# One layer of a diffusion backbone on one core: in the projections with features on partitions, the order of high-part and low-part products within a weight tile

## The chip, the core and the metric

The kernel runs on one core of a Trainium2 chip. Time is device microseconds of one launch; that of the kernel before is the median of three runs. Beside it stands one execution taken by the hardware profiler, from which every duration below is read. The engines are TensorE (PE, with its weight loads PEld), VectorE (DVE), ScalarE (ACT), GpSimd (POOL) and SyncE (SP), which here only issues transfers.

## The reference, cut to what matters

One layer: adaLN (shift, scale and gate from a condition vector), neighbourhood attention over 256 latent tokens and 256 context tokens, output projection, then a gated FFN with a convolution over three tokens; D = 2048, 16 heads, FFN width 5504, all in float32. Only the latent stream is the output.

```python
def conv_ffn(h, w_up, conv_w, conv_b, w_down):
    gate, up = jnp.split(dwconv3(h @ w_up, conv_w, conv_b), 2, axis=-1)
    return (jax.nn.silu(gate) * up) @ w_down

def reference(x, c, ctx, ...):
    sh1, sc1, g1, sh2, sc2, g2 = adaln(cond_lat, w_ada, b_ada)
    h = modulate(rms_norm(x, norm_mix_g), sh1, sc1)
    hc = modulate(rms_norm(ctx, norm_mix_g), csh1, csc1)
    y = neighbourhood_attention(h, hc, w_qkv, q_g, k_g, rpb, w_o, False)
    x = x + g1 * y
    hf = modulate(rms_norm(x, norm_ffn_g), sh2, sc2)
    return x + g2 * conv_ffn(hf, w_up, conv_w, conv_b, w_down)
```

The attention ends with a product with `w_o`. The three products that the change touches are those with `w_o` (2048 x 2048), `w_up` (2048 x 11008) and `w_down` (5504 x 2048).

## The kernel before

**Products in high and low parts.** Every operand of these products is split into an exact high and an exact low part of 12 bits each, and a product of two operands is hi·hi + hi·lo + lo·hi. Activations lie with features on partitions: a block of 128 features holds 512 columns, the 256 tokens' high parts and beside them their low parts. One *wide* product (line 728) multiplies the weight's high part with all 512 columns; one *narrow* product (line 732) multiplies the weight's low part with the 256 columns of high parts, and adds to the first half of the same PSUM bank. One bank belongs to one block of 128 output features.

**Weight tiles.** A tile is 256 rows (two blocks k of 128) by up to 512 columns (four blocks b). `wload` (line 139) has SyncE issue its transfer into one of four slots `wr`; `wpair` (lines 147 to 161) has ScalarE copy it to the rounded high part `wh` (line 155, three slots) and VectorE subtract that from the raw tile to give the low part `wl` (line 156, two slots). `plan` lists all tiles in the order of use; `ahead` (line 180) keeps up to two split, and `weight` hands out the next. So a new `wl` can be written when the tile two before has had its last narrow product.

**The loops.** `proj` (lines 713 to 737) goes over the tiles of a column chunk; within a tile it runs over b, then k, and writes the wide product and then the narrow one. With `fold`, which the last chunk of 256 columns in `w_o` and `w_down` has, the wide product is written as two of 256 columns into the same sums. Three callers: the output projection (the list `WO`; 24 tiles of 512 columns and 16 of 256), the FFN's first product (11 column chunks for the gate and 11 for the up half in turn, 8 tiles each, 160 of them 512 columns wide) and the FFN's second product (the list `DOWN`: three chunks of 512 columns and two of 256, 22 tiles each, the last tile of a chunk with one block k). The banks go round through eight: two `ms`, four `pj`, two `mx`.

**Work beside it.** After each tile `tick` hands out pieces of other work. In the FFN's first product these are the pieces of the chunk before, for each of its four banks: out of PSUM (`drop`, line 828 on VectorE), convolution (lines 838 and 842) and gating (line 855); and the sums of adaLN's last gate (`ada_tasks`), in which ScalarE scales a tile (276) and GpSimd adds it up (277, two sums of 128x512 a tile), or VectorE does both (279). In the second product the pieces are `finish`: two additions and an output transfer for each bank of the finished chunk.

**What sets the order.** The program order is only the start. A scheduler with a model of the times fixes each engine's final order: it lets instructions pass whose inputs it believes ready and holds back others. The slots of the pools set the rest. `hold` makes the first splits of the FFN wait for the second normalization.

Of the kernel before, what the change touches and what calls it, by code (L numbers as in the profile page):

```python
# [15 lines left out]
P = 128  # L16
D = 2048
T = 256
# [9 lines left out]
# pieces of attention per weight tile of the projections beside it  # L28
RATE, RATE3 = 0.46, 0.36
# slots of adaLN weight tiles  # L30
# [4 lines left out]
# columns of the packed small operands  # L35
# [5 lines left out]
# column chunks of the FFN's second product  # L41
DOWN = [(0, 512), (512, 512), (1024, 512), (1536, 256), (1792, 256)]
# blocks of 128 features of the first normalization in steps: (first, number)
GRAINS = [(0, 1), (1, 1)] + [(k, 2) for k in range(2, 16, 2)]
# output projection: (column, columns, first block, last block), the heads of group 3 behind the others
# [5 lines left out]
def block_kernel(  # L51
# [13 lines left out]
    nc = tc.nc  # L65
# [17 lines left out]
    def at():  # L83
        """The four banks of attention in turn."""
        turns.append(0)
        return (ms, mx)[len(turns) % 2]()

    # ---------------------------------------------------------------- constants
# [8 lines left out]
    # window mask over key columns; query column = partition % 64  # L97
    maskt = cp.tile([P, GRID], F32, name="maskt")
    nc.gpsimd.memset(maskt, 0.0)
    for half in range(2):  # L100
        rows = slice(GRID * half, GRID * half + GRID)
        lo = maskt[rows, 0 : GRID - WIN]
# [16 lines left out]
    # adaLN columns by 128-row block: shift / scale of each stream, gates  # L119
# [7 lines left out]
    # relative position rows, each repeated so that a row pitch of 30 shifts it by one column  # L127
# [4 lines left out]
    # ---------------------------------------------------------------- helpers  # L132
    def wload(src, k0, kn, c0, cn, pool=None):
        """Rows of 128-blocks k0..k0+kn and columns c0..c0+cn of a weight."""
# [12 lines left out]
    def wpair(src, k0, kn, c0, cn):  # L147
        """The same rows and columns as exact high and low parts, 12 bits each."""
# [14 lines left out]
    # every weight tile in the order of its use, the next one split ahead of the current one's use  # L163
# [16 lines left out]
    def ahead():  # L180
        """Splits up to two tiles."""
        while plan and len(split) < 2:
            split.append((plan[0], wpair(*plan.popleft())))

    def weight(*tile_):
        """The split parts of the plan's next weight tile."""
        ahead()
        spec, pair = split.popleft()
        assert spec[1:] == tile_[1:]
        return pair  # L190

    def rsqrt_newton(pool, v, n, name, bufs=2):
        """v ** -0.5 for a [P, n] tile, refined once."""
# [11 lines left out]
    def rstd_rows(pool, sums, name, copy):  # L205
        """Sums of squares, [token, block of tokens] -> rstd of each token on every partition."""
# [16 lines left out]
    def col_sums(sums, parts):  # L223
        """sums[t, b]: the sum over partitions of the parts' column b * 128 + t."""
# [9 lines left out]
    class Pieces(deque):  # L234
        """Work handed out in pieces between the products of another part."""
# [16 lines left out]
    def ada_tasks(pool, i, c, dst, gcol=None):  # L252
        """Latent adaLN columns i*D + 512c..: dst[:, 4c..4c+3] = value + b, or (1 + value + b) * g.

        Pairs of a load and its use, and the sum over partitions as a last step: every third tile is
        summed on DVE, the others are scaled on ACT and summed on Pool.
        """
# [45 lines left out]
    def ada_pieces(cols):  # L303
        """Those of several chunks as pieces: loads two tiles ahead, each sum a tile behind."""
# [20 lines left out]
    # ================================================================ attention  # L325
# [29 lines left out]
    def stats(xin, name):  # L355
        """rstd of the tokens of a stream, on every partition."""
# [13 lines left out]
    def nat(psl, tt0, w, kt0, n, first, last):  # L370
        """psl[i] += h[tile tt0 + i, n k-blocks from kt0] @ (split weights), tokens on partitions."""
# [18 lines left out]
    # shift and scale of both streams in steps of one or two 128-row blocks; the first products  # L390
    # of group 0 follow each step
# [3 lines left out]
    def ada_step(b0, nb, work=()):  # L395
        """Blocks b0..b0+nb of the shifts and scales, a piece of the given work ahead of every load."""
# [43 lines left out]
    def modulate(b0, nb, streams=None):  # L440
        """The normalized, scaled and shifted blocks b0..b0+nb as high and low parts."""
# [14 lines left out]
    # sums over steps of the v products of groups 0 and 1  # L456
    vsums = [kv.tile([P, 4, CH], F32, tag=tag, name="vsum") for tag in ("qq", "kl")]

    def first_products(b0, nb):
        """Products with the blocks b0..b0+nb, in six pieces: k of group 0, v of groups 0 and 1."""  # L460
# [54 lines left out]
    def norm_transpose(pt, gcol, dh, dl, t0):  # L515
        """Per-head RMS norm of a [tokens, 4 x 128] product, transposed and split."""
# [55 lines left out]
    def bias(h):  # L572
        """Bias and window of head h: partition = query column, slot = row offset, key column."""
# [16 lines left out]
    def attention(g, q, k, v):  # L590
        """The heads of group g in pieces: scores and softmax, transposes, weighted sums."""
# [86 lines left out]
    def out_of_psum(pts, dst):  # L678
        """The tiles of a projection, where they wait for the end of the group before."""
# [24 lines left out]
    v = []  # L704
# [7 lines left out]
    # ---------------------------------------------------------------- features on partitions  # L712
    def proj(src, kn, c0, cn, mov, tick, k_lo=0, k_hi=None, pts=None, fold=False):
        """src[:, c0:c0+cn].T @ activations: one [128, hi*w | lo*w_hi] bank per 128 columns.

        With fold, the two halves go into the same sums.
        """
        nb = cn // P
        pts = pts or [pj() for _ in range(nb)]
        for k0 in range(k_lo, k_hi or kn, KT):  # L720
            n = min(KT, kn - k0)
            wh, wl = weight(src, k0, n, c0, cn)
            for b in range(nb):
                bs = slice(b * P, (b + 1) * P)
                for k in range(n):
                    kt = k0 + k
                    for t0, t1 in ((0, T), (T, 2 * T)) if fold else ((0, 2 * T),):
                        nc.tensor.matmul(  # L728
                            pts[b][:, : t1 - t0], wh[:, k, bs], mov(kt, slice(t0, t1)),
# [228 lines left out]
```

## Time and profile before

| | |
|---|---|
| time, median of three runs | 1455.89 us (1454.18 to 1458.64) |
| span of the profiled execution | 1455.1 us |
| TensorE busy, products | 1405.5 us, 97%, 7608 products |
| TensorE busy, weight loads | 1166.9 us, 80% |
| VectorE / ScalarE / GpSimd busy | 69% / 54% / 20% |
| HBM | 217 GB/s over the span |
| output projection | from 600 to 705 us |
| second normalization | from 705 to 718 us |
| FFN, first product | from 718 to 1207 us |
| FFN, second product | from 1207 to 1456 us |

A product is recorded from its start to its modelled end, and the next one starts before that end. Rows of the timeline group products of one kind that follow each other (x4 is four); the time of such a row runs from the first one's start to the last one's end. How much TensorE does in a stretch is therefore read from starts, not from busy time. A wait in brackets, as [0.30 <-DVE wl L156], is idle time ahead of the row and the instruction that ended it.

### The profile page before, as it was taken

The numbers are of one execution on the slowest core, as the hardware profiler recorded it, in microseconds if no ns is written. First come the engines' busy times: TensorE is split into PE (matmuls) and PEld (weight loads), VectorE is DVE, ScalarE is ACT, GpSimd is POOL, SyncE is SP. The second block draws the span as 40 slices with busy tenths as digits, with TensorE's granted clock in tenths as the row PEclk, the third lists the DMA queues.
The fourth block names the chain that finished last, engine by engine and source line by source line (L and its number), as shares of the span: only waits on it lengthen the run. The fifth ranks groups of instructions, "written<-read, shape, count | busy, mean of one in ns | idle before, by whom it ended". The sixth has DMA issues, their size and how long they took to land.

```text
span 1455.1 us, 21097 instructions
## 1 busy us (share of the span) xinstructions
PE 1405.5 (97%) x7608; PEld 1166.9 (80%) x7608; DVE 1004.8 (69%) x1541; ACT 782.6 (54%) x1356; POOL 285.2 (20%) x208
## 2 busy tenths in 40 slices
PE   5999999999998999999899999999999999999998
PEld 2665787778787887788788888888888888888888
DVE  4556587687868778766868878788777775545454
ACT  4322265676565676664656656666665654333333
POOL 1000025465445556200201111111111000000000
PEclk9999999999999999999899999999999999999999
DMA  9999547687667777445567776777776556566554
GB/s 308 357 329 319 176 141 250 199 260 220 213 222 246 223 247 244 151 152 175 183 193 230 224 238 222 244 219 228 233 230 193 183 175 206 185 202 205 167 170 156
DMA packets 208920, 317.14 MB, mean 218 GB/s; under 512 B 23360, under 2 KB 87744, under 8 KB 208816
## 3 DMA queue, kind: packets, MB, share of 16 engines
q1 hardware_dynamic: 208688, 315.79, 68.1%
q8 instruction: 59, 0.97, 0.3%
q14 instruction: 45, 0.37, 0.1%
q10 hardware_dynamic: 128, 0.01, 0.0%
HBM read 312.75 MB, written 3.01 MB: 217 GB/s over the span
## 4 chain that ended last, share of the span: by engine, by line
PE 66%; DVE 12%; issue 10%; DMA 7%; ACT 2%; POOL 2%; SPq 1%; DVEq 0%; POOLq 0%; ACTq 0%
PE pj L728 15%; PE pj L732 8%; PE mx L728 7%; PE ms L728 6%; DVE wl L156 4%; PE pj L379 4%; PE pj L378 4%; PE pj L380 4%; DMA wa<-in_w_ada 4%; PE mx L732 4%; PE ms L732 3%; PE ms L411 2%; PE mx L378 2%; PE mx L379 2%; PE mx L380 2%
## 5 line engine op out<-in xcount | busy, mean ns | idle before, releaser
L156 DVE TENSOR_TENSOR wl<-wr,wh 128x1024 fp32r<-128x1024 f32 (+2 forms) x425 | 496.1, 1168 | 257.0 <-PE pj L732 86.8
L155 ACT CAST wh<-wr 128x1024 fp32r<-128x1024 f32 (+2 forms) x425 | 411.8, 970 | 406.0 <-PE pj L728 150.5
L277 POOL TENSOR_TENSOR acc<-acc,wa 128x512 f32<-128x512 f32 x144 | 226.6, 1573 | 440.9 <-issue 218.1
L728 PE MATMUL pj<-hf,wh 128*128 128x512 f32 x688 | 226.7, 397 | 2.0 <-DVE hf L818 2.0
L379 PE MATMUL pj<-wl,hh 128*128 128x512 f32 x512 | 204.8, 400 | 4.6 <-DVE wl L156 4.5
L380 PE MATMUL pj<-wh,hl 128*128 128x512 f32 x512 | 202.0, 397 | 0.0
L378 PE MATMUL pj<-wh,hh 128*128 128x512 f32 x512 | 194.4, 400 | 2.5 <-ACT hh L450 2.5
L732 PE MATMUL pj<-hf,wl 128*128 128x256 f32 x688 | 154.7, 284 | 2.2 <-DVE wl L156 1.7
L732 PEld LDWEIGHTS pj<-hf,wl 128*128 128x128 f32 x688 | 130.6, 190 | 20.6 <-DVE wl L156 6.2
L728 PEld LDWEIGHTS pj<-hf,wh 128*128 128x128 f32 x688 | 125.3, 190 | 17.7 <-DVE hf L818 2.8
L276 ACT ACTIVATE wa<-wa,sT 128x512 f32<-128x512 f32 x144 | 97.4, 718 | 77.7 <-DMA wa<-in_w_ada 68.1
L728 PE MATMUL mx<-hf,wh 128*128 128x512 f32 x352 | 124.1, 393 | 0.0
L379 PEld LDWEIGHTS pj<-wl,hh 128*128 128x128 f32 x512 | 97.8, 191 | 28.7 <-DVE wl L156 7.9
L728 PE MATMUL ms<-hf,wh 128*128 128x512 f32 x336 | 120.1, 396 | 0.0
L378 PEld LDWEIGHTS pj<-wh,hh 128*128 128x128 f32 x512 | 96.8, 190 | 27.0 <-ACT hh L450 3.4
L380 PEld LDWEIGHTS pj<-wh,hl 128*128 128x128 f32 x512 | 97.6, 191 | 19.5
L732 PE MATMUL mx<-hf,wl 128*128 128x256 f32 x352 | 84.8, 282 | 1.5 <-DVE wl L156 1.5
L279 DVE SCALAR_TENSOR_TENSOR acc<-wa,sT,acc 128x512 f32<-128x512 f32 x80 | 74.4, 931 | 10.7 <-DMA wa<-in_w_ada 10.1
L732 PE MATMUL ms<-hf,wl 128*128 128x256 f32 x336 | 81.7, 282 | 0.0
L732 PEld LDWEIGHTS mx<-hf,wl 128*128 128x128 f32 x352 | 66.3, 188 | 10.4 <-DVE wl L156 3.2
L732 PEld LDWEIGHTS ms<-hf,wl 128*128 128x128 f32 x336 | 63.3, 188 | 7.8
L728 PEld LDWEIGHTS ms<-hf,wh 128*128 128x128 f32 x336 | 63.2, 188 | 6.9
(251 smaller groups left out, 2384.7 us busy)
## 6 DMA issues: line engine op xcount, KB each, us to landing
wr<-in_w_up SPq DMA_DIRECT2D x160, 512.0 KB, 4.4
wa<-in_w_ada SPq DMA_DIRECT2D x128, 512.0 KB, 4.7
wr<-in_w_qkv SPq DMA_DIRECT2D x93, 512.0 KB, 4.9
wr<-in_w_down SPq DMA_DIRECT2D x63, 512.0 KB, 4.6
wx<-in_w_ada SPq DMA_DIRECT2D x56, 512.0 KB, 8.7
wr<-in_w_o SPq DMA_DIRECT2D x24, 512.0 KB, 3.8
wr<-in_w_down SPq DMA_DIRECT2D x45, 256.0 KB, 3.0
wr<-in_w_up SPq DMA_DIRECT2D x16, 384.0 KB, 3.4
```

The source lines that it names most:

```text
L155: a = nc.scalar.copy(hi[:, :kn, :cn], w[:, :kn, :cn])
L156: b = nc.vector.tensor_tensor(out=lo[:, :kn, :cn], in0=w[:, :kn, :cn], in1=hi[:, :kn, :cn].bitcast(F32), op=ALU.subtract,)
L276: nc.scalar.mul(w[:, k, :], w[:, k, :], s)
L277: nc.gpsimd.tensor_add(acc, acc, w[:, k, :])
L279: nc.vector.scalar_tensor_tensor(out=acc, in0=w[:, k, :], scalar=s, in1=acc, op0=ALU.mult, op1=ALU.add)
L378: nc.tensor.matmul(pt, hh[:, kt, ts], wh[:, k, :], start=a, stop=False)
L379: nc.tensor.matmul(pt, hh[:, kt, ts], wl[:, k, :], start=False, stop=False)
L380: nc.tensor.matmul(pt, hl(kt, ts), wh[:, k, :], start=False, stop=z)
L411: nc.tensor.matmul(ap_[32 * k : 32 * k + 32, :n], s32[:, 4 * q + k, :], w[:, k * n : (k + 1) * n], start=(q == 0), stop=(q == 3), tile_pos ...
L728: nc.tensor.matmul(pts[b][:, : t1 - t0], wh[:, k, bs], mov(kt, slice(t0, t1)), start=(kt == 0 and t0 == 0), stop=False,)
L732: nc.tensor.matmul(pts[b][:, :T], wl[:, k, bs], mov(kt, slice(0, T)), start=False, stop=(kt == kn - 1),)
```

## The change

In `proj`, the loop over the cells of a tile is run twice: first all wide products of the tile (for each b, both k), then all narrow ones in the same order of cells. Operands, sums, banks, splits, transfers and `tick` stay. The rest of the diff blanks comments, which moves line numbers by one behind `proj`: the wide product is line 727 afterwards, the narrow one 733, `drop` 829, the convolution 839 and 843, the gating 856.

```diff
     def proj(src, kn, c0, cn, mov, tick, k_lo=0, k_hi=None, pts=None, fold=False):
...
             wh, wl = weight(src, k0, n, c0, cn)
-            for b in range(nb):
-                bs = slice(b * P, (b + 1) * P)
-                for k in range(n):
-                    kt = k0 + k
-                    for t0, t1 in ((0, T), (T, 2 * T)) if fold else ((0, 2 * T),):
-                        nc.tensor.matmul(
-                            pts[b][:, : t1 - t0], wh[:, k, bs], mov(kt, slice(t0, t1)),
-                            start=(kt == 0 and t0 == 0), stop=False,
-                        )
+            cells = [(b, slice(b * P, (b + 1) * P), k) for b in range(nb) for k in range(n)]
+            for b, bs, k in cells:
+                kt = k0 + k
+                for t0, t1 in ((0, T), (T, 2 * T)) if fold else ((0, 2 * T),):
                     nc.tensor.matmul(
-                        pts[b][:, :T], wl[:, k, bs], mov(kt, slice(0, T)), start=False,
-                        stop=(kt == kn - 1),
+                        pts[b][:, : t1 - t0], wh[:, k, bs], mov(kt, slice(t0, t1)),
+                        start=(kt == 0 and t0 == 0), stop=False,
                     )
+            for b, bs, k in cells:
+                kt = k0 + k
+                nc.tensor.matmul(
+                    pts[b][:, :T], wl[:, k, bs], mov(kt, slice(0, T)), start=False,
+                    stop=(kt == kn - 1),
+                )
             tick()
```

**Three places in the built order.** In these rows the names are the program's tiles: `hf` is the FFN's input, `act_*` the activated features, `pj`, `ms` and `mx` the banks; x4 is four such instructions in a row.

TensorE, FFN's first product, where one chunk ends in its `pj` banks and the next begins in `mx` and `ms`. Before:

```order
L728 MATMUL pj<-hf,wh 128x512 x4
L728 MATMUL mx<-hf,wh 128x512 x2
L728 MATMUL ms<-hf,wh 128x512 x2
L732 MATMUL pj<-hf,wl 128x256
L728 MATMUL pj<-hf,wh 128x512
L732 MATMUL pj<-hf,wl 128x256 x2
L728 MATMUL pj<-hf,wh 128x512
```

After:

```order
L727 MATMUL pj<-hf,wh 128x512 x8
L727 MATMUL mx<-hf,wh 128x512
L733 MATMUL pj<-hf,wl 128x256 x8
L727 MATMUL mx<-hf,wh 128x512 x3
L727 MATMUL ms<-hf,wh 128x512 x4
L733 MATMUL mx<-hf,wl 128x256 x4
L733 MATMUL ms<-hf,wl 128x256 x4
```

Before, the scheduler had moved four wide products of a tile ahead and let the others alternate with the narrow ones; now all eight stand ahead of the eight narrow ones.

VectorE, FFN's first product, from the split of one tile of a chunk (`wl_9318`) to that of the next (`wl_9350`). Before:

```order
L156 TENSOR_TENSOR wl_9318<-wr_9315,wh_9317 128x1024
L842 SCALAR_TENSOR_TENSOR y_9337<-z_9308,sm_69,y_9337 128x255
L838 SCALAR_TENSOR_TENSOR y_9373<-z_9312,sm_69,y_9373 128x255
L828 TENSOR_TENSOR z_9403<-ms_9054,t_9402 128x256
L855 TENSOR_TENSOR y_9337<-y_9337,gt_9169 128x256
L838 SCALAR_TENSOR_TENSOR y_9428<-z_9370,sm_69,y_9428 128x255
L842 SCALAR_TENSOR_TENSOR y_9373<-z_9312,sm_69,y_9373 128x255
L156 TENSOR_TENSOR wl_9350<-wr_9347,wh_9349 128x1024
```

After:

```order
L156 TENSOR_TENSOR wl_9318<-wr_9315,wh_9317 128x1024
L839 SCALAR_TENSOR_TENSOR y_9337<-z_9308,sm_69,y_9337 128x255
L829 TENSOR_TENSOR z_9403<-ms_9054,t_9402 128x256
L843 SCALAR_TENSOR_TENSOR y_9337<-z_9308,sm_69,y_9337 128x255
L839 SCALAR_TENSOR_TENSOR y_9373<-z_9312,sm_69,y_9373 128x255
L839 SCALAR_TENSOR_TENSOR y_9428<-z_9370,sm_69,y_9428 128x255
L856 TENSOR_TENSOR y_9337<-y_9337,gt_9169 128x256
L156 TENSOR_TENSOR wl_9350<-wr_9347,wh_9349 128x1024
```

Six pieces stand between the two splits in both; they are two 838, two 842, one 828 and one 855 before, and three 839, one 843, one 829 and one 856 now.

TensorE, FFN's second product, the hand-over from its third chunk of columns (`pj`) to its fourth (`mx`). Before:

```order
L728 MATMUL pj<-act_fp,wh 128x512 x4
L728 MATMUL mx<-act_row_6466,wh 128x512 x2
L732 MATMUL pj<-act_fp,wl 128x256 x4
L732 MATMUL mx<-act_row_6466,wl 128x256
L728 MATMUL mx<-act_row_6466,wh 128x512
L732 MATMUL mx<-act_row_6466,wl 128x256 x2
```

After:

```order
L727 MATMUL pj<-act_fp,wh 128x512 x4
L727 MATMUL mx<-act_row_6466,wh 128x512 x3
L733 MATMUL pj<-act_fp,wl 128x256 x4
L727 MATMUL mx<-act_row_6466,wh 128x512
L733 MATMUL mx<-act_row_6466,wl 128x256 x4
```

The old chunk's last four narrow products stand behind three wide ones of the next chunk instead of two.

## Rows read from the trace of the kernel before

**Rows 1.** Page, part 1: busy us (share of the span) x instructions.

```profile
PE 1405.5 (97%) x7608; PEld 1166.9 (80%) x7608; DVE 1004.8 (69%) x1541; ACT 782.6 (54%) x1356; POOL 285.2 (20%) x208
```

**Rows 2.** Windows: stretch; its us; busy of PE, PEld, DVE, ACT, POOL; PEclk; DMA; GB/s.

```profile
718.00:1207.00 489.00, 485.30 (x2757) 420.49 (x2756) 382.06 (x557) 301.06 (x470) 63.68 (x40) 1.00 0.68 214
```

**Rows 3.** Timeline of TensorE, 903.6 to 908.9: start us, us, instruction [idle before].

```profile
903.66 1.08 PE L728 MATMUL pj<-hf,wh 128*128 128x512 f32 x4
904.58 0.28 PE L732 MATMUL pj<-hf,wl 128*128 128x256 f32 x1
904.69 0.40 PE L728 MATMUL pj<-hf,wh 128*128 128x512 f32 x1
...
906.47 1.08 PE L728 MATMUL pj<-hf,wh 128*128 128x512 f32 x4
907.86 0.39 PE L732 MATMUL pj<-hf,wl 128*128 128x256 f32 x1 [0.30 <-DVE wl L156]
908.08 0.40 PE L728 MATMUL pj<-hf,wh 128*128 128x512 f32 x1
```

**Rows 4.** Waits of weight loads by stage (us, times, longest); the last from their timeline.

```profile
PEld ms L732 <- DVE wl L156: 1.4, 2, 0.8
...
PEld pj L732 <- DVE wl L156: 6.2, 10, 0.9
PEld mx L732 <- DVE wl L156: 3.2, 4, 0.8
...
PEld mx L732 <- DVE wl L156: 1.6, 3, 0.6
...
907.86 0.19 PEld L732 LDWEIGHTS pj<-hf,wl 128*128 128x128 f32 x1 [0.74 <-DVE wl L156]
```

**Rows 5.** Timeline of VectorE, 901 to 907.

```profile
901.12 1.22 DVE L156 TENSOR_TENSOR wl<-wr,wh 128x1024 fp32r<-128x1024 f32 x1
902.26 1.52 DVE L842 SCALAR_TENSOR_TENSOR y<-z,sm,y 128x255 f32<-128x255 f32 x1
903.70 1.51 DVE L838 SCALAR_TENSOR_TENSOR y<-z,sm,y 128x255 f32<-128x255 f32 x1
905.14 0.41 DVE L828 TENSOR_TENSOR z<-ms,t 128x256 f32<-128x256 f32 x1
905.48 0.41 DVE L855 TENSOR_TENSOR y<-y,gt 128x256 f32<-128x256 f32 x1
905.81 0.47 DVE L838 SCALAR_TENSOR_TENSOR y<-z,sm,y 128x255 f32<-128x255 f32 x1
906.20 0.47 DVE L842 SCALAR_TENSOR_TENSOR y<-z,sm,y 128x255 f32<-128x255 f32 x1
906.60 1.21 DVE L156 TENSOR_TENSOR wl<-wr,wh 128x1024 fp32r<-128x1024 f32 x1
```

**Rows 6.** Timeline of GpSimd, 900 to 908.

```profile
901.28 3.66 POOL L277 TENSOR_TENSOR acc<-acc,wa 128x512 f32<-128x512 f32 x2 [19.42 <-issue]
```

**Rows 7.** Timeline of TensorE in the second FFN product, 1265 and 1408.

```profile
1265.40 1.09 PE L728 MATMUL pj<-act_fp,wh 128*128 128x512 f32 x4
1266.33 0.64 PE L732 MATMUL pj<-act_fp,wl 128*128 128x256 f32 x4
1266.81 0.63 PE L728 MATMUL mx<-act_row,wh 128*128 128x512 f32 x2
...
1408.33 0.63 PE L728 MATMUL mx<-act_fp,wh 128*128 128x512 f32 x2
...
1409.75 0.63 PE L728 MATMUL mx<-act_fp,wh 128*128 128x512 f32 x2
```

**Rows 8.** Timeline of TensorE, 895.2 to 897.6: eight wide products, then a narrow one.

```profile
895.26 0.62 PE L728 MATMUL mx<-hf,wh 128*128 128x512 f32 x2
...
897.10 0.28 PE L732 MATMUL mx<-hf,wl 128*128 128x256 f32 x1
```

**Rows 9.** Timeline of TensorE, 1397 to 1401.

```profile
1399.56 0.73 PE L728 MATMUL mx<-act_row,wh 128*128 128x512 f32 x2 [0.96 <-ACT wh L155]
```

## The prediction, made before the result was known

> **What bounds the kernel now.** I read the page first: TensorE is busy 97% of the span with 7608 products [rows 1], and the windows by stage say the same of the long stage of the FFN's first product: 485 of 489 us, with the granted clock at full speed and VectorE at 382 us [rows 2]. Ends of products are modelled, so this busy time hides short stalls. I therefore read TensorE by the starts in its timeline: how far one product starts behind the one before.
>
> A tile of this stage has eight wide products (512 columns, high part) and eight narrow ones (256 columns, low part); the scheduler has put four wide ones ahead. In the tile that starts at 903.66 nothing waits: the first narrow product comes 0.92 us behind the first wide one (0.23 us a product), the next product 0.11 us later, the next tile 2.81 us later [rows 3]. That next tile, at 906.47, is the same, but its first narrow product comes 1.39 us behind, held by the VectorE instruction that makes the low part (L156), and the product behind it takes 0.22 instead of 0.11 [rows 3]. This stall costs 0.47 + 0.11 = 0.58 us. The waits of the weight loads count such places: 2 in the output projection (1.4 us), 10 and 4 in the first FFN product (6.2 and 3.2), 3 in the second (1.6); the one of 906.47 stands there as 0.74 us [rows 4]. So a recorded wait is worth 0.58/0.74 = 0.78 of itself: 16 places and 10.8 us ahead of the second FFN product are 8.4 us of TensorE, the other three 1.2 us.
>
> Why VectorE is late: [rows 5] are its instructions from one split to the next. The split for the tile of 906.47 stands, in VectorE's order, behind six pieces of the chunk before. Two of these took 1.52 and 1.51 us, where the same kind takes 0.47, while GpSimd ran two sums of adaLN [rows 5, 6]. So 4.3 us pass between the end of one split (902.34) and the start of the next (906.60).
>
> **The change part by part.** Nothing is added or removed: the same products, loads, splits and transfers. The order moves.
>
> *The low part is wanted later.* The built order has eight wide products, then eight narrow ones, so the first narrow one comes at 8 x 0.23 = 1.84 us of its tile instead of 0.92. What else VectorE may do between two splits follows: from the end of the tile that frees the first split's buffer there are two tiles (5.62 us) and then 0.92 or 1.84 us to the need, and two splits take 2 x 1.22. That leaves 4.1 us now and 5.0 us after. [Rows 5] need 4.3, and the first split started at 901.12, 0.27 us behind its tile's start (906.47 - 5.62 = 900.85): 0.47 us late, as the products say. After the change VectorE's order has three L838, one L842, one L828 and one L855 between the same two splits: 4 x 0.47 + 2 x 0.41 = 2.7 us, and with two sums of GpSimd among them 2 x 1.05 more, 4.8 us. With the 0.27 that is 5.1 against 5.0: it just fits, within a tenth. The other places now wait as long or less (at most 0.9 us recorded, 0.7 by the ratio) and gain the same 0.92 us. I take 90% of the 8.4 us: **-7.5 us**. Bounds: half stays, -4.2; all goes, -8.4. What is late next in these stages is only the products' own spacing.
>
> The Trainium skill speaks to the 1.05 us (SBUF — State Buffer, "Who interferes with whom"): a VectorE instruction with two SBUF inputs contends with a GpSimd instruction that reads SBUF, and the one that starts first holds the shared pair for its whole length while the other fully blocks. The trace agrees in kind: 1.52 and 1.51 us where 0.47 is usual. By that rule the change takes none of these blocks away, it only leaves time to suffer them, and a third one between two splits would cost its full length again, which is the slower rival below.
>
> *Spacing.* Does a group of eight cost what the alternation costs where nothing waits? A tile of one block in the second FFN product already runs four wide and then four narrow: 1265.40 to 1266.81 is 1.41 us, 0.48 of it for the four narrow ones [rows 7]. The same number of each in alternation takes 1408.33 to 1409.75, 1.42 us [rows 7]. Where two tiles meet, eight wide ones follow each other, 20 times, in 1.82 to 1.84 us (895.26 to 897.10) [rows 8]. A grouped tile is then 1.83 + 2 x 0.48 = 2.79 us against 2.80 to 2.81. I take -13 ns. There are 24 such tiles in the output projection, 160 in the first FFN product, 63 in the second: 247 x 13 ns = **-3.2 us**. Bounds: 1.84 + 0.97 = 2.81, nothing; and, if narrow ones come nearer to the 0.11 us of a single one [rows 3], 0.118 each, 1.83 + 0.94 = 2.77, -10 us. I stay by the runs of four, which are closest to a run of eight.
>
> The Trainium skill (TensorE: Matmul & The Clock Gate, "Back-to-back issue gap") makes the gap a matter of the product's own columns, N/2.4 + 2.5 ns, 216 and 109 ns here, whatever stands beside it; the trace has about 230 and 120. By that rule this term is zero and the sum is -7.2 us.
>
> *The second FFN product.* Its three short stalls stand where a finished chunk of four banks is handed over; a little behind them TensorE waits 0.96 us for the ACT split of a tile that had not landed [rows 9]. VectorE's eight additions of the finished chunk start when its banks are done, and on SyncE's queue the output transfers and the next weight loads follow these. The built order has three wide products of the next chunk ahead of the old chunk's last narrow ones where two stood: the banks are done 0.23 us later. The three stalls are covered, but the wait for the landing takes their place. I put it at **+0.3 us**; bounds -2.2 (all of it goes: 1.2 and 1.0) and +1.
>
> *At no cost.* The high part's buffer comes back earlier by the eight narrow products; ACT's split had time already, so nothing follows. The low part's buffer comes back at the tile's end, as now, so VectorE's splits, the slots of the raw weights and their transfers keep their times. A finished chunk's banks are dropped later, but the next chunk has four others. The kernel's last tile stands as before, and all of TensorE's order ahead of the output projection is unchanged.
>
> Sum: -7.5 - 3.2 + 0.3 = -10.4 us. Against the profiled execution's span, 1455.1, that is 1444.7; the median of the three runs, 1455.9, lies 0.8 us above the span, so **1445.5 us**.
>
> **The rivals.**
> - *Order is free.* A tile takes the same time in either order, and only the waits go: 1455.9 - 7.5 + 0.3 = 1448.7 us. For it: 1.41 against 1.42 us is one last digit [rows 7]. Against it: wide products come at 0.23 in a run of eight at most [rows 8], and between narrow ones no closer [rows 3]. The Trainium skill's rule on gaps above is this case.
> - *The lateness moves along.* The pieces between two splits leave a tenth of a microsecond; every further wait for ACT among them makes the split late again. Then 70% of the stalls stay: 1455.9 - 2.5 + 0.3 is 1453.7 without a gain from spacing, about 1451 with it; I price it at 1453. For it: the 5.1 against 5.0 above.
> - *Slower.* A third sum of GpSimd falls between the splits of a chunk's third and fourth tile: 2.7 + 3 x 1.05 = 5.9 us, 0.9 over the 5.0 from which it decides, and 0.1 for the product behind. At 22 chunks that is +22 us; less 8.4 and 3.2 it gives 1466 us. For it: drops and convolutions now stand closer together there. Against it: the sums come in pairs, 19.42 us of idle time apart [rows 6], and not every chunk has one there.
> - *More.* Narrow products at 0.118 us and a free hand-over: 1455.9 - 8.4 - 10 - 2.2 = 1435 us. Against it: 0.48 us for four [rows 7].
> That the change does nothing is excluded: the built order is different in every tile.
>
> **How the numbers follow.** A difference under about 0.3% (4.4 us, so a time over 1451.5) can't be told from no change. Forecast 0.54 (1441 to 1450), order is free 0.15, moving along 0.16, slower 0.07, more 0.08. Faster by over 0.3%: nearly all of the first two and "more", with a little of "moving along", 0.75; within it: the rest, 0.18; slower: 0.07. The range 1439 to 1453.5 leaves out the slower case, most of "more" and the upper end of "moving along", together not quite 0.2.
>
> **What would show it.** Right: the waits of the low part's weight loads on L156 fall from 12.4 us to under 2.5; from a tile's first wide product to its first narrow one it is 1.84 us nearly everywhere; tiles start 2.79 us apart. Spacing wrong: undisturbed tiles at 2.81 or more, or near 2.77. Moving along: waits on L156 of the old size, behind 1.9 us or more of wide products. Slower: three VectorE instructions lengthened by 1 us between two splits. The prediction is wrong altogether if eight narrow products in a row take clearly more than 0.96 us, or if ACT's or VectorE's splits wait for something that isn't in these rows.

## The result, and the profile after

The changed kernel takes **1447.6 us** (median of eight runs, 1445.9 to 1449.9), the one before 1455.0 beside it (eight runs, 1452.0 to 1458.6). The ratio is 0.9945, with a 95% interval of 0.9929 to 0.9962: 8.0 us, and between 5.5 and 10.3. The forecast was 1445.5, 10.4 us less.

The profiled execution's span fell from 1455.1 to 1444.0 us, by 11.1, which is more than the medians say. The timeline of TensorE tells where. I divide it at the first product that reads `om` (output projection), `hf` (first FFN product) and `act` (second), and at the end of its last product:

| us | up to the output projection | to the FFN | first FFN product | second FFN product |
|---|---|---|---|---|
| before | 603.5 | 109.4 | 492.0 | 246.5 |
| after | 601.0 | 110.6 | 484.6 | 244.2 |
| difference | -2.6 | +1.2 | -7.4 | -2.3 |

The FFN's first product starts at 712.9 us before, earlier than the 718 of the table of stages before. The first column is the same order of TensorE's instructions in both kernels. In the eleven other executions below with that order (e8 alone has another) it took 599.9 to 607.1 us: the 2.6 us are scatter. What the change did is in the other three columns, -8.5 us, and that agrees with the runs.

The boundary between the two FFN products does not part equal work. When the first product that reads `act` runs, the old order still has three wide and six narrow products of the first FFN product to come, 1.40 us by their starts; the grouped order has six narrow ones, 0.71 us; e4, e7 and e10 have none. TensorE there, before and then after:

```profile
1204.94 1.08 PE L728 MATMUL pj<-act_row,wh 128*128 128x512 f32 x4
...
1207.15 0.28 PE L732 MATMUL ms<-hf,wl 128*128 128x256 f32 x1
```

```profile
1196.11 1.52 PE L727 MATMUL pj<-act_row,wh 128*128 128x512 f32 x6
...
1197.94 0.40 PE L733 MATMUL ms<-hf,wl 128*128 128x256 f32 x2
```

*On equal work*, with these counted where they belong, the first FFN product takes 493.4 and 485.3 us, 8.1 less, and the second 245.1 and 243.5, 1.6 less. Stage times below go by the first product, as in the expectations, unless they are called on equal work.

The page of the profile after, part 4 (the chain that ended last, by engine):

```profile
PE 74%; issue 9%; DMA 5%; DVE 4%; ACT 3%; POOL 2%; SPq 1%; DVEq 0%; POOLq 0%; ACTq 0%
```

TensorE is busy 97% of the span as before [rows 1], which says next to nothing. The chain says more: VectorE holds 4% of it, where it held 12%. The waits of the weight loads after, for the output projection, the first and the second FFN product (us, times, longest):

```profile
PEld ms L733 <- DVE wl L156: 0.8, 1, 0.8
...
PEld mx L733 <- DVE wl L156: 0.4, 1, 0.4
...
PEld mx L733 <- DVE wl L156: 1.1, 3, 0.5
PEld mx L727 <- ACT wh L155: 0.4, 1, 0.4
```

On L156 they were 1.4, 9.4 and 1.6 us [rows 4]; now they are 0.8, 0.4 and 1.1. A place like that of [rows 3, 5, 6], after: TensorE, VectorE and GpSimd in their timelines.

```profile
896.31 2.00 PE L727 MATMUL pj<-hf,wh 128*128 128x512 f32 x8
898.15 1.12 PE L733 MATMUL pj<-hf,wl 128*128 128x256 f32 x8
899.10 2.00 PE L727 MATMUL pj<-hf,wh 128*128 128x512 f32 x8
900.94 1.11 PE L733 MATMUL pj<-hf,wl 128*128 128x256 f32 x8
```

```profile
896.51 2.33 DVE L156 TENSOR_TENSOR wl<-wr,wh 128x1024 fp32r<-128x1024 f32 x1
```

```profile
894.57 3.19 POOL L277 TENSOR_TENSOR acc<-acc,wa 128x512 f32<-128x512 f32 x2 [19.16 <-issue]
```

From the first wide product to the first narrow one it is 1.84 us, and from tile to tile 2.79. GpSimd's pair still lengthens VectorE: here it hits the split itself, 2.33 us where 1.21 is usual. The split ends at 898.84; its tile's low part is first wanted at 900.94. The delay is still there, and nobody waits for it.

Here only one instruction of VectorE was lengthened: three `drop`s, which read a bank, ran beside GpSimd's pair at 0.38 to 0.41 us each. The tightest places of the stage have two lengthened pieces between two splits. VectorE at one of them, and the weight load that wants the low part:

```profile
906.61 1.51 DVE L843 SCALAR_TENSOR_TENSOR y<-z,sm,y 128x255 f32<-128x255 f32 x1
908.04 1.51 DVE L858 TENSOR_TENSOR act_row<-y,act_row 128x256 fp32r<-128x256 f32 x1
...
910.14 1.21 DVE L156 TENSOR_TENSOR wl<-wr,wh 128x1024 fp32r<-128x1024 f32 x1
...
911.89 1.13 PEld L733 LDWEIGHTS pj<-hf,wl 128*128 128x128 f32 x8
```

The split ends at 911.35, 0.54 us before that load starts. In the whole stage the kernel before has 12 places with two instructions lengthened from the end of one split to the end of the next (the second split may be one of them), and the weight load waits at all 12. The changed kernel has 8, and the low part is done 0.5 to 2.1 us ahead of its load at each.

### The profile page after: what moved, and what is told of

It is laid out like the page before. It is cut to its first block, busy times and chain, and to the rows that moved or that the text cites. A ratio compares the mean times of both kernels' runs of the same rounds, so it can differ in the third digit from the quotient of the medians.

```text
span 1444.0 us, 21091 instructions
## 1 busy us (share of the span) xinstructions
PE 1399.1 (97%) x7608; PEld 1167.8 (81%) x7608; DVE 1000.0 (69%) x1541; ACT 778.5 (54%) x1356; POOL 281.1 (19%) x208
## 4 chain that ended last, share of the span: by engine, by line
PE 74%; issue 9%; DMA 5%; DVE 4%; ACT 3%; POOL 2%; SPq 1%; DVEq 0%; POOLq 0%; ACTq 0%
PE pj L727 18%; PE pj L733 9%; PE mx L727 8%; PE ms L727 7%; PE pj L379 5%; PE pj L378 5%; PE pj L380 5%; PE mx L733 4%; PE ms L733 4%; DMA wa<-in_w_ada 3%; PE ms L411 2%; PE mx L378 2%; PE mx L379 2%; PE mx L380 2%; POOL acc L277 2%
## 5 line engine op out<-in xcount | busy, mean ns | idle before, releaser
L156 DVE TENSOR_TENSOR wl<-wr,wh 128x1024 fp32r<-128x1024 f32 (+2 forms) x425 | 503.8, 1186 | 280.6 <-PE pj L733 106.3
L727 PE MATMUL pj<-hf,wh 128*128 128x512 f32 x688 | 176.3, 396 | 2.0 <-DVE hf L819 2.0
L733 PEld LDWEIGHTS pj<-hf,wl 128*128 128x128 f32 x688 | 94.6, 192 | 6.8
L733 PE MATMUL pj<-hf,wl 128*128 128x256 f32 x688 | 97.8, 285 | 0.0
L727 PE MATMUL mx<-hf,wh 128*128 128x512 f32 x352 | 97.7, 394 | 0.0
L727 PE MATMUL ms<-hf,wh 128*128 128x512 f32 x336 | 90.9, 390 | 0.0
L727 PEld LDWEIGHTS mx<-hf,wh 128*128 128x128 f32 x352 | 60.6, 190 | 7.8
L478 DVE TENSOR_TENSOR vsum<-vsum,mx 128x512 f32<-128x512 f32 x64 | 43.2, 684 | 34.2 <-PE mx L380 34.0
L733 PEld LDWEIGHTS mx<-hf,wl 128*128 128x128 f32 x352 | 53.7, 189 | 7.1 <-DVE wl L156 0.4
L584 POOL TENSOR_TENSOR bt<-bt,maskt 128x384 f32<-128x384 f32 x16 | 17.9, 1123 | 206.4 <-DMA bt<-rpd 173.7
```

The source lines that it names most:

```text
L156: b = nc.vector.tensor_tensor(out=lo[:, :kn, :cn], in0=w[:, :kn, :cn], in1=hi[:, :kn, :cn].bitcast(F32), op=ALU.subtract,)
L478: nc.vector.tensor_add(acc[:, h0 + i, :], acc[:, h0 + i, :], pr_[i])
L727: nc.tensor.matmul(pts[b][:, : t1 - t0], wh[:, k, bs], mov(kt, slice(t0, t1)), start=(kt == 0 and t0 == 0), stop=False,)
L733: nc.tensor.matmul(pts[b][:, :T], wl[:, k, bs], mov(kt, slice(0, T)), start=False, stop=(kt == kn - 1),)
```

## Experiments

### Taking GpSimd's sums away: e1 and e2

The theory (A): the stalls come from VectorE's pieces, lengthened while GpSimd adds, and the later need covers them; besides, the new order itself is some 13 ns a tile cheaper. The rival (B): the order of the products is what costs. Both kernels lose the same line:

```diff
                 elif pool_:
                     nc.scalar.mul(w[:, k, :], w[:, k, :], s)
-                    nc.gpsimd.tensor_add(acc, acc, w[:, k, :])
+                    if i != 5:
+                        nc.gpsimd.tensor_add(acc, acc, w[:, k, :])
```

> The kernel before, with GpSimd's sums of adaLN's last gate left out (line 277 for this gate alone; its transfers, ScalarE's scaling and VectorE's sums stay, so that the gate is incomplete). TensorE's order is that of before. Theory A (two terms: VectorE's splits are late in the first FFN product because GpSimd's sums lengthen its pieces, some 6 us; and the grouped order has 15 ns less a tile): weight loads wait on L156 under 1.5 us in the first FFN product instead of 9.4; that stage takes 486 us instead of 492; tiles stay 2.81 us apart; time about 1449. Theory B (the order of the products is what costs, and the splits are late whatever GpSimd does): waits of 7 us or more remain, the stage takes 490 or more, time 1453 to 1456.

> The changed kernel with the same sums left out. Theory A: next to e1_before_no_sums only the spacing is left: first FFN product 2.3 us shorter than there (160 tiles x 15 ns), second some 1.5 to 2 us, time about 3.5 us less, near 1446; next to the changed kernel with its sums no more than 0.5 us in the first FFN product. Theory B: 7 us or more below e1_before_no_sums.

e1 took 1450.1 us (ratio 0.9955, 0.9938 to 0.9972). Its first FFN product took 485.6 us, and the waits on L156 there fell from 9.4 to 1.0:

```profile
PEld pj L733 <- DVE wl L156: 1.0, 2, 0.8
```

One of VectorE's two kinds of convolution pieces in this stage (count, busy us, mean ns), first in the kernel before, then in e1, where the lines are one further; the other kind has 578 and 479 ns:

```profile
L838 DVE SCALAR_TENSOR_TENSOR y<-z,sm,y 128x255 f32<-128x255 f32 x83 | 46.8, 576 | 0.6 <-ACT y L835 0.6
```

```profile
L839 DVE SCALAR_TENSOR_TENSOR y<-z,sm,y 128x255 f32<-128x255 f32 x83 | 38.7, 479 | 1.7 <-ACT y L836 1.6
```

The same instructions take 479 ns on average instead of 577 when GpSimd does not add, and the stalls go with that. TensorE's order is that of before, word for word, so B falls. e2 took 1446.2 us. Its first FFN product is 483.3 us, 2.3 less than e1 (3.0 on equal work): the rest of the stalls, the spacing, and 0.6 us in the stage's first 7 us. Next to the changed kernel it is 1.3 less, where 0.5 at most was expected. Of that, 1.1 us lie in those first 7 us. Behind the second normalization the granted clock is still 0.50 (1.2 GHz), in e2 for the first 3.4 us of the stage, in the changed kernel for the first 5.8. The second FFN product of e2 was not 1.5 to 2 us shorter than e1's but 0.2 (245.3 and 245.4), and on equal work it was 0.5 longer: in e2 a weight load waits 1.5 us there for ScalarE's split, in e1 none does.

### More of the same: e11 and e12

Each of the same sums made twice (the loop around the line is `for _ in range(1 + (i == 5))`), in the changed kernel and in the one before; one execution each.

> The changed kernel with each of GpSimd's sums of adaLN's last gate made twice (the gate is then wrong; everything else, and TensorE's order, stays). Asks how much room the later need leaves. By the prediction's account there is a tenth of a microsecond between two splits with two lengthened pieces; with four, 2 x 1.05 us more, the split would be 2 us late at each of the places that were stalls before: weight loads wait on L156 15 to 30 us in the first FFN product, which takes 500 us or more instead of 484.5. If the room is wider than that account says (pieces of VectorE that need not stand there, lengthened pieces that fall elsewhere): waits under 8 us, 485 to 492 us.

> The kernel before with the same sums made twice. Theory A: the stalls grow by what the further lengthened pieces cost, 1 us a piece where a split follows: waits on L156 of 20 us or more in the first FFN product instead of 9.4, the stage 500 us or more instead of 492, and always more than in the changed kernel with the same sums, by 6 us or more. Rival (lateness is not from GpSimd): 9 to 10 us and 492 as before.

Waits of the weight loads in the first FFN product, e11 and then e12:

```profile
PEld pj L734 <- DVE wl L156: 14.6, 8, 3.1
...
PEld mx L734 <- DVE wl L156: 0.7, 3, 0.2
```

```profile
PEld pj L733 <- DVE wl L156: 12.3, 9, 2.6
PEld mx L733 <- DVE wl L156: 10.2, 4, 2.5
```

15.3 and 22.5 us; the stage takes 502.6 and 510.4 us, the span 1467.8 and 1472.2. So the later need does not remove the cause. In the changed kernel it gave room for two lengthened pieces between two splits, with 0.5 us left at the tightest place; with four the stalls are back, longer than before. One such place of e11, VectorE between two splits:

```profile
821.44 1.21 DVE L156 TENSOR_TENSOR wl<-wr,wh 128x1024 fp32r<-128x1024 f32 x1
822.58 1.52 DVE L844 SCALAR_TENSOR_TENSOR y<-z,sm,y 128x255 f32<-128x255 f32 x1
824.02 1.51 DVE L859 TENSOR_TENSOR act_row<-y,act_row 128x256 fp32r<-128x256 f32 x1
825.45 1.51 DVE L857 TENSOR_TENSOR y<-y,gt 128x256 f32<-128x256 f32 x1
826.88 1.48 DVE L859 TENSOR_TENSOR act_row<-y,act_row 128x256 fp32r<-128x256 f32 x1
828.29 1.21 DVE L156 TENSOR_TENSOR wl<-wr,wh 128x1024 fp32r<-128x1024 f32 x1
```

Four pieces, four sums of GpSimd, each piece 1.05 to 1.1 us longer than usual.

### One stage alone: e3 and e5

The two loops for one weight only; elsewhere each group is a single cell, which is the order of before. e6 is the kernel before once more, for the scatter; e5 and e6 are one execution each.

```diff
+            groups = [cells] if src is w_up else [[x] for x in cells]
```

> The two loops for the first FFN product alone; the output projection and the second FFN product have the order of before. Theory A: first FFN product 484.6 us as in the changed kernel, second 246.5 as before, from the output projection to the FFN 109.4 as before (110.6 in the changed kernel), time 1447 to 1448. Rival (the grouping in the output projection costs the 1.2 us seen there, by shifting attention's last pieces): this kernel is 1 us faster there than the changed one; if that stretch is 110.6 here too, the 1.2 us are scatter of executions.

> The two loops for the output projection alone; both FFN products have the order of before. From the first product of the output projection to the first of the FFN the kernels with the old order took 109.4, 109.8, 110.3 and 110.6 us, the two with the grouped one 110.6 and 110.9. Theory A (grouping gains nothing there, since the stage ends behind attention's last pieces and a few late operands, not behind L156): 110 to 111 us; the first FFN product 492 us and 9 us of waits on L156, as before; span 1455 to 1457. Rival (the prediction's term: 1.0 us of stalls and 0.3 of spacing go): under 109 us.

> The kernel before once more, for the scatter of a stage between two executions. All theories: first FFN product within 0.5 us of 492.0; up to the output projection anything from 600 to 604 us, as the runs of one order so far; output projection to FFN 109.4 to 110.6. Waits on L156 in the first FFN product 9 us or more again.

e3 took 1449.1 us (ratio 0.9951, 0.9934 to 0.9967): 484.2 us in the first FFN product, 247.0 in the second. So nearly the whole gain of the change is in the first FFN product. Its 110.3 us from the output projection to the FFN decided nothing by itself. e5 has 111.2 there, so the rival (under 109) falls, 492.1 in the first FFN product, and a span of 1456.7. e6 has 109.6, 492.1 and 246.9.

All executions with either order together, e9 and e10 with their further edit left out: from the output projection to the FFN the old order took 109.4, 109.4, 109.6, 109.8, 110.3 and 110.6 us (before, e12, e6, e1, e3, e4), the grouped one 110.6, 110.6, 110.7, 110.9 and 111.2 (e7, after, e11, e2, e5). Grouping costs 0.9 us there on average. In the second FFN product the old order with two slots took 245.4 to 247.0 (six executions), the grouped one 244.2 to 246.0 (five); on equal work the means are 245.05 and 244.27.

### Where the output projection loses it: e9 and e10

In every one of these executions but e8's the last product of the output projection starts 101.4 to 101.5 us behind its first. The difference between the two orders lies behind it. Before, then after: ScalarE's and VectorE's instructions there, and TensorE's wait for the sums of the second normalization.

```profile
702.75 1.05 ACT L155 CAST wh<-wr 128x1024 fp32r<-128x1024 f32 x1 [1.27 <-DMA wr<-in_w_up]
...
703.92 1.23 DVE L156 TENSOR_TENSOR wl<-wr,wh 128x1024 fp32r<-128x1024 f32 x1 [0.75 <-PE ms L732]
705.06 0.87 DVE L778 SCALAR_TENSOR_TENSOR x<-ms,g1T,x 128x256 f32<-128x256 f32 x2
...
705.60 0.61 PE L227 MATMUL ms<-ones,sacc 128*128 128x1 f32 x4 [0.33 <-DVE x L778]
```

```profile
701.44 1.05 ACT L155 CAST wh<-wr 128x1024 fp32r<-128x1024 f32 x1 [1.35 <-DMA wr<-in_w_up]
...
702.52 1.23 DVE L156 TENSOR_TENSOR wl<-wr,wh 128x1024 fp32r<-128x1024 f32 x1 [1.71 <-PE ms L733]
703.66 0.87 DVE L779 SCALAR_TENSOR_TENSOR x<-ms,g1T,x 128x256 f32<-128x256 f32 x2
...
704.19 0.49 PE L227 MATMUL ms<-ones,sacc 128*128 128x1 f32 x3 [1.47 <-DVE x L779]
```

In both kernels the low part of the FFN's first tile stands, in VectorE's order, ahead of the last two additions of the output projection. Before, it runs beside the last products and is done as they end. After, the last products are through at 702.7, the split starts at 702.52 behind ScalarE's, and the additions come 1.1 us late. ScalarE's split starts when the tile's transfer has landed. SyncE issues this transfer 95.3 to 95.4 us behind the stage's first product in the six executions with the old order here, and 95.7 in all seven with the grouped one (e9 and e10 included, e8 left out); it lands 3.7 to 4.7 and 4.0 to 5.1 us later. From the end of the stage's last product to the normalization's first sum it is then 0.3 to 1.2 us with the old order and 1.2 to 1.9 with the grouped one, e9 and e10 left out. So 0.3 us of the delay come with the order in every execution; why the transfers then take as long as they do the runs don't tell.

So e9 has this tile handed to the splits only once `hold` is set; e10 is the same with the three slots of e7.

```diff
-        while plan and len(split) < 2:
+        while plan and len(split) < 2 and (plan[0][0] is not w_up or hold):
```

> The changed kernel, with the split of the FFN's first tile issued behind the second normalization's first steps like that of the second tile, and so in VectorE's order behind the last two additions of the output projection (line 779). Theory A (this split stands ahead of the additions in the changed kernel and holds the sums of the normalization 1.2 to 1.9 us): the wait of TensorE for these sums on line 779 falls to about 0.3 us; from the output projection's first product to the FFN's first 109.4 us instead of 110.6; the FFN products as in the changed kernel; time 1 us less, 1446 to 1447. Rival (VectorE does the split later, between the normalization's steps, and the features come later by its 1.2 us): 110.5 us or more, time 1447 to 1449.

> The same with three slots for the low parts from the second normalization on (e7_after_three_low_slots). Theory A: stages as there, but 109.4 us instead of 110.6 from the output projection to the FFN; 1441 to 1442.5. Rival: 110.5 us there, no change against 1442.7.

TensorE's waits there, e9 and then e10:

```profile
PE pj L727 <- DVE hf L819: 2.3, 1, 2.3
...
PE ms L227 <- DVE x L779: 0.3, 1, 0.3
```

```profile
PE pj L728 <- DVE hf L821: 3.5, 1, 3.5
...
PE ms L228 <- DVE x L780: 0.3, 1, 0.3
```

The wait for the sums falls from 1.5 to 0.3 us, as expected, and the stretch to 109.8 in e9. In e10 the split only moved: the first product of the FFN waits 3.5 us for its features instead of 2.3 in e7, and the stretch is 110.9, as the rival said. The times, 1447.9 (ratio 0.9932, 0.9914 to 0.9950) and 1444.7 us (0.9920, 0.9903 to 0.9938), can't be told from those of the kernels without this edit. The place is shown; a gain is not.

### A third slot for the low part: e4 and e7

The other way to cover a late split is to let it start a tile earlier. From the second normalization on the low parts come from a pool with three slots; e4 has the program order of before, e7 that of the change.

```diff
-        lo = wp.tile([P, KT, CH], F32R, tag="wl", name="wl", bufs=2)
+        lo = lows[-1][0].tile([P, KT, CH], F32R, tag="wl", name="wl", bufs=lows[-1][1])
...
     fp = ctx.enter_context(tc.tile_pool(name="fp", bufs=1))
+    lows.append((fp, 3))
```

> The kernel before with three slots instead of two for the low parts from the second normalization on; program order of the products as before. The built order then alternates strictly, wide and narrow. Theory A: a split may be done a tile earlier, so waits on L156 in both FFN products fall to under 1 us; strict alternation costs 8 x (234 + 118.5) = 2.82 us a tile; first FFN product 492 - 7.1 + 1.8 = 486.7 us, time about 1449 to 1450. Theory B (a slot does not matter, the order of products does): first FFN product 491 or more, time 1454 or more.

> The changed kernel with three slots for the low parts from the second normalization on. Theory A: nothing is left to gain in the first FFN product but 0.2 us (483.7 to 484.5 us); in the second the stalls at the hand-over go, 1 us, and the 4.6 us that e4_three_low_slots gained there come back in part: 242 to 243 us. Time 1445 to 1447, the same as e4_three_low_slots within what can be measured. Rival (spacing and stalls add up further): first FFN product under 482, time under 1443.

e4 took 1447.2 us (ratio 0.9934, 0.9916 to 0.9952): no weight load waits for either split in the first FFN product, 485.1 us, and one, for 0.2 us, in the second, 241.9. On equal work that is 8.3 and 3.2 us less than before. So a slot does what the later need does, with the old program order, and more in the second product, where the stalls of the hand-over nearly go too. What missed was the price of alternation, and the built order: only some 100 of the 160 full tiles alternate strictly, and most others have four wide products ahead, as before. Its timeline at two tiles, each from its first wide product to that of the next tile, with wide and narrow in strict turn between them:

```profile
849.67 0.39 PE L729 MATMUL pj<-hf,wh 128*128 128x512 f32 x1
...
852.44 0.39 PE L729 MATMUL pj<-hf,wh 128*128 128x512 f32 x1
...
893.78 0.40 PE L729 MATMUL pj<-hf,wh 128*128 128x512 f32 x1
...
896.60 0.40 PE L729 MATMUL pj<-hf,wh 128*128 128x512 f32 x1
```

The same order takes 2.77 us in one stretch and 2.81 in another (2.82 here by the rounded starts). Of the undisturbed tiles in strict turn 44 take 2.77 us and 54 take 2.81; the mean over the stage is near 2.80.

e7 took **1442.7 us** (ratio 0.9909, 0.9892 to 0.9926), the lowest of all here: 483.9 and 241.5 us in the FFN products, without a wait on either split. It is better than expected by 2 us, and below the changed kernel by about 0.4%; their intervals just don't meet. The rival's time (under 1443) came true, its first FFN product (under 482) did not; but on equal work this stage is 1.4 us shorter than in the changed kernel, where 0.2 was expected, and the second FFN product 2.0.

### The same order in the other projections: e8

```diff
                 nc.tensor.matmul(pt, hh[:, kt, ts], wh[:, k, :], start=a, stop=False)
-                nc.tensor.matmul(pt, hh[:, kt, ts], wl[:, k, :], start=False, stop=False)
-                nc.tensor.matmul(pt, hl(kt, ts), wh[:, k, :], start=False, stop=z)
-            side.tick(side.rate)
+                nc.tensor.matmul(pt, hl(kt, ts), wh[:, k, :], start=False, stop=False)
+            side.tick(side.rate / 2)
+        for i, pt in enumerate(psl):
...
+                nc.tensor.matmul(pt, hh[:, kt, ts], wl[:, k, :], start=False, stop=z)
+            side.tick(side.rate / 2)
```

> The changed kernel, and the same regrouping in the projections with tokens on partitions: of each tile all products with the high part first, then those with the low part (lines 378 to 380 before). There TensorE waited 3.4 us for L156 at 4 places in the changed kernel, 4.5 us at 6 in the one before. If lateness of the split is what costs there too: these waits fall under 1 us, the part ahead of the output projection takes 597 to 600 us, time 1445 to 1446. If the transfers set that part (DMA share 0.77 there) or attention's pieces shift: within 2 us of the changed kernel, 1446 to 1450, or slower.

1460.8 us (ratio 1.0030, 1.0017 to 1.0044): slower than the kernel before, and 13 us over the changed one. Up to the output projection it takes 614.6 us. TensorE's waits there, e8 and then the kernel before (e6):

```profile
PE mx L538 <- DVE qn L532: 5.8, 3, 2.5
PE pj L386 <- DVE wl L156: 5.7, 4, 2.8
...
PE ms L654 <- DVE ptl L642: 2.4, 1, 2.4
```

```profile
PE ms L532 <- DVE qn L526: 4.0, 3, 1.5
PE pj L379 <- DVE wl L156: 3.5, 5, 1.5
...
PE mx L532 <- DVE qn L526: 2.2, 2, 1.4
```

The low part is waited for longer, not shorter: 5.7 us against 3.5. The waits for `qn` have not grown in e8 (5.8 us against 4.0 and 2.2), but others for pieces of attention have, as the 2.4 us for `ptl`; the places of these pieces between the products have moved as well. All of TensorE's waits in this part add up to 45 us in e8 and 36 in e6. What comes first isn't settled: the edit also splits each hand-out of pieces in two, and no run separates that.

## Why the prediction was right, step by step

**The stalls in the first FFN product: right in cause and size.** The forecast put 90% of 9.4 us recorded waits at 0.78, which is 6.6 us. Start to start, losses of over 60 ns between products of this stage, its first 7 us left out, add up to 7.5 us before and 0.8 after: 6.7 us. In the first 7 us, part of them at 1.2 GHz, the changed kernel loses 0.5 us more; such starts differ by 1.1 us between executions of the grouped order alone (e2), so this is not shown to come from the change. That the later need covers two lengthened pieces is shown, at 8 places. "Just fits, within a tenth" was not: the room left was 0.5 us or more. At [rows 5]'s place, for which that tenth was worked out, GpSimd's pair now runs one split earlier, beside `drop`s and the split itself, and at the tightest places only four pieces stand between the splits, not six. So the worst case of that account, six pieces with two of them lengthened, did not come about, and that is luck. The sentence of the Trainium skill (SBUF — State Buffer, "Who interferes with whom") held as it was used: the changed kernel keeps the blocks, 2.33 us for a split, and has time to suffer them.

**Spacing: the size nearly, the reason not.** Tiles are 2.79 us apart as forecast, and the stage's spacing is 1.65 us less by the same count (forecast 2.1). But e4 shows that grouped and alternating are no two prices: strict alternation runs at 2.77 or 2.81. The order of before, four wide ones ahead and the rest in turn, at 2.80 to 2.81, was on the dear side of this. What sets the two prices no run shows. The Trainium skill's formula for the gap (TensorE: Matmul & The Clock Gate, "Back-to-back issue gap"), N/2.4 + 2.5 ns, depends on a product's columns alone, and the section calls it the gap of an isolated product. For 512 columns it gives about 216 ns, where the traces have 230 to 232, and it does not give two values for one order either.

**The output projection: the step that failed.** Its share of the sum was -1.3 us (1.0 of stalls, 0.3 of spacing). It measured +0.9 on average, and +1.2 in this pair. One of the two stalls did go, but in the first part of the stage a wait of 0.45 us for attention's last features took its place; and at the end the split of the next stage's first tile got into the way of the last additions. I wrote that VectorE's splits and the transfers of the raw weights keep their times, and that a finished chunk's banks being done later costs nothing, since the next chunk has four others. That holds where a chunk of the same kind follows. At the end of a stage there is none, and whatever stands in VectorE's order ahead of the last additions is on the path. ScalarE's split comes at 100.5 us of the stage instead of 99.2 since it follows the landing of its transfer, which is issued 0.3 us later; the rest of this delay stays open.

**The second FFN product: +0.3, less 0.8 of spacing, against -1.6 in this pair on equal work and -0.8 on average** (245.05 in six executions with the old order, 244.27 in five with the grouped one). I had the three stalls covered and the landing wait in their place. In fact most of the stalls stayed (1.1 of 1.6 us), and the landing wait goes its own way: 1.0 us before, 0.2 after by TensorE's own count (before in [rows 9], after here):

```profile
1388.67 1.18 PE L727 MATMUL mx<-act_row,wh 128*128 128x512 f32 x4 [0.21 <-ACT wh L155]
```

As waits of the weight load these are 1.3 and 0.4 us; it was 1.6 us in e6, 1.8 in e3 and 1.5 in e2, in either order.

**The sum.** -10.4 forecast. By stages -8.5 in this pair; by the runs -8.0. The 2 us between are the sum of three misses on equal work: the output projection 2.5 us short (+1.2 for -1.3), the first FFN product 0.6 short (-8.1 for -8.7), and the second 1.1 better than forecast (-1.6 for -0.5). That the last made up for part of the first is luck. Of the rivals, that order is free gave 1448.7, which lies 1.1 us from the measured time, nearer than the forecast's 1445.5; but its reason is not what happened: spacing did gain, and the output projection took it back. Moving along and the slower case did not happen. With 0.5 us left at the tightest places, a third lengthened piece there, about 1.05 us, would by these figures have brought stalls back.

## What to carry to other kernels

Where the operand that comes last serves a part of a tile's products, put those last: within the long stage it cost nothing here, and it gives the engine that makes the operand the time of the others. It covers lateness only up to that time, so count what else stands between two of its instructions; a further buffer does the same without a new order, and both together did best here. Look at the ends of the stages separately: there the work that finishes last has no successor to hide behind, and the same order, put into the projections beside attention with the hand-out of pieces halved, cost 13 us.

## What was not expected of the hardware

A long stall can cost more than its length. Behind one stall of e11 TensorE's next products come slowly. Its timeline, and the granted clock in two windows, behind this stall and behind another of the same length (the stretch, its us, busy times, then the clock):

```profile
824.87 2.00 PE L728 MATMUL pj<-hf,wh 128*128 128x512 f32 x8
829.56 1.24 PE L734 MATMUL pj<-hf,wl 128*128 128x256 f32 x8 [2.68 <-DVE wl L156]
830.61 3.57 PE L728 MATMUL pj<-hf,wh 128*128 128x512 f32 x8
```

```profile
830.61:834.00 3.39, 3.39 (x10) 2.63 (x9) 1.50 (x2) 0.11 (x1) 0.00 (x0) 0.50 0.99 326
924.30:927.80 3.50, 3.44 (x20) 3.07 (x21) 2.60 (x3) 1.05 (x1) 0.00 (x0) 1.00 0.65 212
```

Eight wide products take 3.57 us where they took 2.00; the granted clock in this stretch is 0.50, that is 1.2 instead of 2.4 GHz. It does not always come so: behind the stall that ended at 924.36, 2.68 us too, the clock stays at 1.00. It fell behind three of the four such stalls of this stage in e11, behind three of the eight of 2.1 us in e12, and behind none in the kernel before, where TensorE's idle time was 0.45 us at most. What decides it these runs don't show. The 15.3 us of waits in e11 cost 18.8 us of starts, where in the kernel before 9.4 us of waits, none over 0.9, cost 7.5. And the two spacings of one alternating order, 2.77 and 2.81 us a tile, each kept for several tiles on end, are measured and not explained.
